# Global attention: softmax weights transposed in 32x32 blocks by VectorE and by DMA through DRAM, in place of TensorE

## The chip, the core and the metric

The kernel runs on one core of a Trainium2 chip. The metric is the device time of one execution in microseconds. The kernel before takes 859.36 us (median of 3 runs, 859.27 to 859.72). The core has TensorE (PE, its weight loads shown apart as PEld), VectorE (DVE), ScalarE (ACT), GpSimd (POOL) and SyncE (SP), which here issues nearly all DMAs. Each engine takes its instructions in one fixed order, and an instruction that waits holds up all behind it on that engine.

## The reference

Two layers of a hybrid encoder over 512 grid tokens and 16 meta tokens, width 1024. Each layer has one input projection, whose columns feed a global attention branch, a windowed attention branch, a gate for each, and two merge gates:

```python
def attend(qb):                                   # global branch: 8 heads, 2 kv heads, width 64
    s = jnp.einsum('bqkgd,bskd->bkgqs', qb, k).astype(jnp.float32) * scale
    p = jax.nn.softmax(s, axis=-1).astype(v.dtype)
    return jnp.einsum('bkgqs,bskd->bqkgd', p, v)
...
oa = gqa_attention(qa, ka, va) * jax.nn.silu(za)
ob = neighbourhood_attention(qb, kb, vb, rpb) * jax.nn.silu(zb)
ya = jnp.einsum('ble,ed->bld', oa, w_o_attn)
yb = jnp.einsum('ble,ed->bld', ob, w_o_na)
mixed = jax.nn.sigmoid(ga) * ya + jax.nn.sigmoid(gb) * yb
return x + jnp.einsum('bld,de->ble', mixed, w_out)
```

The change is in `attend`: between the softmax `p`, which has queries on the partitions, and the product with `v`, which needs the keys there.

## The kernel before, in words

Activations lie with features on the partitions and tokens along the free dimension. Every large product is done with three float32r matmuls: a value is split into a high part (a rounding copy) and a low part (what is left), and high x high, high x low and low x high are accumulated (lines 325 to 327 in `product`). A weight chunk comes in two halves of 256 KB. For each half SP loads `raw`, ACT casts it to `whi`, POOL subtracts to get `wlo`; each of the three has 4 buffers, so a load waits until POOL is done with the half four places earlier.

The projections and merge products are the main stream of TensorE. Attention work is threaded into it by two `Side` objects. `product` calls `tick()` after each of its spans (about 24 matmuls in layer 0); each tick moves the branches one step, and every fourth tick a new unit of global attention begins. So two or three units are in flight. `GQA_AT` says at which tick of a unit each step is emitted, for layer 0 and layer 1.

A unit of global attention is one head and 256 queries (two parts of 128): 16 units in each layer, and 2 in layer 0 for the 64 meta queries of a kv head. Its steps before:

- `scores(i)`: TensorE computes S (lines 556, 557), VectorE scales it, takes the maximum and writes it to SBUF (L807), ScalarE exponentiates (L811), VectorE multiplies by the reciprocal sum (L813). The weights P of a part are 128 queries x 528 keys, and both parts share the tile `both` of 1056 columns.
- `transposes(kt)`: four 128x128 transpositions on TensorE into a PSUM bank `pt` (L129), then `split`: ScalarE casts the bank to `pth`, VectorE subtracts to get `ptl` (L193, L194). Two such steps for a unit, 8 transpositions.
- `meta_transposes`: one narrow transposition of the 32 columns of meta keys into `ptm`, split by two casts and two subtractions into the padded tile `ga`.
- `sums`: 9 matmuls of `VA2` with `pth`, `ptl` and `ga` into `av` (L854).

`VA2` is V with tokens on the partitions: `scaled` writes V of all heads (`va`) from PSUM, and `values` transposes it.

The framework gives each instruction its place in its engine's queue by priorities and its own estimate of times, so the table sets the emission and the queue orders follow from it.

Of the kernel before, what the change touches and what calls it, by code (L numbers as in the profile page):

```python
# [11 lines left out]
F32 = mybir.dt.float32  # L12
# [6 lines left out]
P = 128  # L19
# [3 lines left out]
NREAL = GW * GH  # L23
# [13 lines left out]
GQA_AT = ({"scores": (0, 2), "transposes": (3, 4), "meta": 5, "sums": (5, 7)},  # L37
          {"scores": (0, 1), "transposes": (3, 6), "meta": 6, "sums": (5, 7)})
# [57 lines left out]
def trunk_kernel(ctx: ExitStack, tc: tile.TileContext, xT, w, gn, gf, bias, rope, out):  # L96
# [357 lines left out]
    for l in range(DEPTH):  # L454
# [264 lines left out]
        def values(v, out, tiles, name):  # L719

            n = tiles[0][2]
            ps = bank(ps_t, f"vt{name}", "tp")
            for i, (u, a, _) in enumerate(tiles):
                nc.tensor.transpose(ps[:n, P * i:P * (i + 1)], v[:, a:a + n], ident)
            u, e = tiles[0][0], len(tiles)
            src = ps[:n, :P * e].rearrange("p (t h d) -> p t h d", t=e, h=2)
            split(out[:n, u:u + e, :, 0], out[:n, u:u + e, :, 1], src)
            if n < P:
                nc.gpsimd.memset(out[:NMETA, u].rearrange("p h s d -> p (h s d)").bitcast(F32), 0.0)
                nc.scalar.copy(out[n:2 * n, u:u + e], out[:n, u:u + e].bitcast(F32))  # L730
# [15 lines left out]
        side_gqa.later(NORM_AT[l]["values"][1], lambda v=v, VA2=VA2: values(v, VA2, [(4, NTOK - 32, 64)], f"am{l}"))  # L746
# [68 lines left out]
        def global_unit(kv, parts, n, name, done):  # L815
# [41 lines left out]

            steps = [(at, lambda i=i: scores(i)) for i, at in zip(range(len(parts)), GQA_AT[l]["scores"])]
            n_t = 4 // per
            for i, (at, then) in enumerate(zip(GQA_AT[l]["transposes"][:n_t], GQA_AT[l]["sums"][-n_t:])):  # L860
                steps.append((at, lambda kt=per * i: transposes(kt)))
                f = 2 * per * (i + 1)
                steps.append((then, lambda a=2 * per * i, b=f + (f == 8): sums(a, b)))
            steps.append((GQA_AT[l]["meta"], meta_transposes))
# [391 lines left out]
```

## Time and profile before

| quantity | value |
|---|---|
| median of 3 runs | 859.36 us |
| the profiled execution: its time, its span | 859.04 us, 857.3 us |
| PE busy, share of the span | 847.7 us, 99% |
| PEld busy | 788.7 us, 92% |
| DVE busy | 533.7 us, 62% |
| ACT busy | 492.4 us, 57% |
| POOL busy | 352.7 us, 41% |
| mean granted TensorE clock | 0.998 |
| DMA moved | 95.55 MB in 64670 packets |
| queue q1, share of 16 DMA engines | 37.5% |
| PE's part in the chain that ended last | 93% |

The span runs from the first to the last instruction of the profiled execution; 1.7 us of its time lie outside. Busy time is the union of an engine's instructions. Matmuls overlap (one of 264 columns is shown as lasting some 0.29 us, and the next starts 0.12 us after it), so the cost of a matmul on PE is read from the distance between starts.

### The profile page before, as it was taken

What the parts mean: (1) busy time and instruction counts of PE and PEld (TensorE: products, weight loads), DVE (VectorE), ACT (ScalarE), POOL (GpSimd) and SP (SyncE); (2) the same over time, 40 slices, a digit from 0 to 9 for tenths busy, and PEclk for the clock granted to TensorE, in tenths of its full rate; (3) what the DMA queues carried; (4) which work ended last, traced back from release to release, by engine and by line L of the source; (5) the groups of instructions that cost most, each with busy time, mean ns of one, the idle gap of its engine ahead of it and who ended that gap; (6) DMA issues with size and microseconds to landing.
All of it is one profiled execution on the core that took longest, in us unless ns stands there. A gap on an engine that the chain in (4) does not pass through costs nothing.

```text
span 857.3 us, 16238 instructions
## 1 busy us (share of the span) xinstructions
PE 847.7 (99%) x5960; PEld 788.7 (92%) x5960; DVE 533.7 (62%) x1310; ACT 492.4 (57%) x1169; POOL 352.7 (41%) x279
## 2 busy tenths in 40 slices
PE   9999999999999999999999999999999999999997
PEld 9999999999999999999998999999988888888786
DVE  7975667777774673436448656677768545454633
ACT  8654777667864564334445556577758555543422
POOL 2663343333233233454764653334333333344851
PEclk9999999999999999999999999999999999999999
DMA  7384334335122212334655654334442222223502
GB/s 251 94 220 125 100 114 126 94 97 132 50 60 65 75 63 64 117 93 146 155 134 135 173 167 132 108 99 140 123 119 75 81 79 76 86 86 121 174 13 99
DMA packets 64670, 95.55 MB, mean 111 GB/s; under 512 B 22864, under 2 KB 23888, under 8 KB 64592
## 3 DMA queue, kind: packets, MB, share of 16 engines
q1 hardware_dynamic: 63872, 93.46, 37.5%
q8 instruction: 47, 0.77, 0.4%
q10 hardware_dynamic: 720, 1.06, 0.3%
q14 instruction: 31, 0.25, 0.1%
HBM read 76.72 MB, written 4.19 MB: 94 GB/s over the span
## 4 chain that ended last, share of the span: by engine, by line
PE 93%; ACT 3%; DVE 2%; issue 1%; DMA 1%; SPq 0%; POOLq 0%; POOL 0%; ACTq 0%; DVEq 0%
PE pp L327 19%; PE pp L325 19%; PE pp L326 19%; PE av L854 4%; PE y L327 4%; PE y L325 4%; PE y L326 4%; PE pt L129 3%; PE avb L997 2%; PE S L556 2%; PE S L557 2%; PE pf L1175 2%; PE pf L1177 2%; PE pf L1176 2%; PE Sb L557 1%
## 5 line engine op out<-in xcount | busy, mean ns | idle before, releaser
L241 POOL TENSOR_TENSOR wlo<-raw,whi 128x512 fp32r<-128x512 f32 x210 | 280.3, 1338 | 451.9 <-ACT whi L240 375.5
L325 PE MATMUL pp<-hh,whi 128*128 128x264 f32 (+1 forms) x1040 | 330.1, 317 | 0.0
L327 PE MATMUL pp<-hh,wlo 128*128 128x264 f32 (+1 forms) x1040 | 324.8, 312 | 0.0
L326 PE MATMUL pp<-hl,whi 128*128 128x264 f32 (+1 forms) x1040 | 323.9, 311 | 0.0
L240 ACT CAST whi<-raw 128x512 fp32r<-128x512 f32 x210 | 129.2, 619 | 151.8 <-issue 53.6
L327 PEld LDWEIGHTS pp<-hh,wlo 128*128 128x128 f32 x1040 | 195.8, 188 | 10.7
L326 PEld LDWEIGHTS pp<-hl,whi 128*128 128x128 f32 x1040 | 196.5, 189 | 9.0
L325 PEld LDWEIGHTS pp<-hh,whi 128*128 128x128 f32 x1040 | 196.1, 189 | 8.8
L807 DVE CUSTOM_DVE_ANT_1 P<-S,r 128x528 f32<-128x528 f32 x64 | 45.1, 705 | 18.5 <-PE S L557 17.5
L194 DVE TENSOR_TENSOR ptl<-pt,pth 128x512 fp32r<-128x512 f32 x64 | 44.0, 689 | 17.4 <-ACT pth L193 16.7
L1072 DVE TENSOR_TENSOR mg<-pp,rbc 128x264 f32<-128x264 f32 (+1 forms) x48 | 24.8, 517 | 41.9 <-PE pp L327 41.7
L811 ACT ACTIVATE P<-P,st 128x528 f32<-128x528 f32 x64 | 47.2, 737 | 2.0
L932 ACT ACTIVATE bias<-bias,stb 128x208 f32<-128x208 f32 (+1 forms) x64 | 31.1, 486 | 21.6 <-DVE stb L930 21.2
L193 ACT CAST pth<-pt 128x512 fp32r<-128x512 f32 x64 | 37.2, 583 | 4.4 <-PE pt L129 3.2
L129 PE MATMUL pt<-ident,P 128*128 128x128 f32 x256 | 39.2, 275 | 0.4 <-DVE ptl L194 0.4
L1073 ACT ACTIVATE mg<-mg 128x264 f32<-128x264 f32 (+1 forms) x48 | 23.7, 494 | 25.8 <-DVE mg L1072 25.8
L326 PE MATMUL pp<-mx,whi 128*128 128x264 f32 x128 | 36.6, 286 | 0.0
L325 PE MATMUL pp<-mx,whi 128*128 128x264 f32 x128 | 36.5, 285 | 0.0
L327 PE MATMUL pp<-mx,wlo 128*128 128x264 f32 x128 | 36.3, 284 | 0.0
L813 DVE TENSOR_SCALAR P<-P,st 128x528 f32<-128x528 f32 x64 | 34.1, 533 | 2.1
L854 PE MATMUL av<-pth,VA 128*128 128x256 f32 x128 | 35.4, 299 | 0.0
L854 PE MATMUL av<-ptl,VA 128*128 128x256 f32 x128 | 33.0, 280 | 0.0
(539 smaller groups left out, 1771.5 us busy)
## 6 DMA issues: line engine op xcount, KB each, us to landing
raw<-in_w_dram SPq DMA_DIRECT2D x210, 256.0 KB, 2.7
bias<-in_bias_dram SPq DMA_DIRECT2D x16, 480.0 KB, 4.2
KB<-KB SPq DMA_DIRECT2D x24, 272.0 KB, 3.7
rawl<-in_w_dram SPq DMA_DIRECT2D x16, 256.0 KB, 3.0
x<-in_xT_dram SPq DMA_DIRECT2D x8, 264.0 KB, 4.6
xr<-in_xT_dram SPq DMA_DIRECT2D x8, 264.0 KB, 3.7
Q<-q SPq DMA_DIRECT2D x16, 128.0 KB, 2.8
x1d<-xt SPq DMA_DIRECT2D x32, 64.0 KB, 3.0
```

What stands on the lines that cost most here:

```text
L129: nc.tensor.transpose(ps, src, ident[:n, :n])
L193: split_at["hi"] = nc.scalar.copy(hi, src)
L194: split_at["any"] = nc.vector.tensor_sub(lo, src, hi.bitcast(F32))
L240: cast = nc.scalar.copy(hi, raw)
L241: sub = nc.gpsimd.tensor_sub(lo, raw, hi.bitcast(F32))
L325: nc.tensor.matmul(ps, wh, rh[:, a:b], start=i == 0, stop=False)
L326: nc.tensor.matmul(ps, wh, rl[:, a:b], start=False, stop=False)
L327: nc.tensor.matmul(ps, wl, rh[:, a:b], start=False, stop=i == n - 1)
L807: newest["max"] = nc.vector.tensor_tensor_reduce(p[:n].rearrange("p (i k) -> p i k", i=2), S[:n, :, :HALF], scale[:n].unsqueeze(2).to_broa ...
L811: nc.scalar.activation(p[:n], p[:n], AF.Exp, bias=st[:n, 1:2], scale=1.0, accum_out=st[:n, 2:3])
L813: nc.vector.tensor_scalar_mul(p[:n], p[:n], st[:n, 3:4])
L854: nc.tensor.matmul(c["av"], rows2(c["t"][i][0]), c["t"][i][1], start=i == 0, stop=i == 8)
```

## The change

Each unit now does without TensorE between the softmax and `sums`:

- `turn(i)`: VectorE transposes part i within 32x32 blocks, in place (128x512 for part 0, 128x544 for part 1, which takes the 32 meta columns along; 64x544 for the meta queries, after a GpSimd memset of 16 columns). After part 1 SP stores the whole tile to DRAM (`there`, 540 KB, rows of 4224 bytes).
- `back`: SP loads it back into the same tile in four DMAs of 32 partitions each, in pieces of 512 bytes, so that blocks land on the partitions of their keys; a fifth DMA fetches the meta block (`meta`, pieces of 128 bytes).
- `split_part` and `split_ends` make `pth`, `ptl` and `ga` as before, but read SBUF in place of PSUM, `pth` and `ptl` through a view with runs of 32 elements.
- The keys come in another order, so `scaled` writes the columns of `va` permuted, with spans of 256 and 272 columns in place of 264 and 264, and the zeros for the meta values come with it (the memset in `values` goes).
- The table: in layer 0 `sums` moves from ticks (5, 7) to (6, 7), the two splits from (3, 4) to (5, 5); in layer 1 from (3, 6) to (5, 5).

```diff
-GQA_AT = ({"scores": (0, 2), "transposes": (3, 4), "meta": 5, "sums": (5, 7)},
-          {"scores": (0, 1), "transposes": (3, 6), "meta": 6, "sums": (5, 7)})
+GQA_AT = ({"scores": (0, 2), "turn": (1, 3), "back": 4, "split": (5, 5), "ends": 5, "sums": (6, 7)},
+          {"scores": (0, 1), "turn": (1, 2), "back": 3, "split": (5, 5), "ends": 5, "sums": (6, 7)})
...
         def scaled(c, name):
             t = slots.tile([P, 960], F32, tag="bias", bufs=2, name=name)
-            for ps, a, b in project(c, True):
-                evac["v"] = nc.vector.tensor_mul(t[:, a:b], ps, rbc[:, a:b])
-
-            nc.vector.tensor_mul(t[:, NTOK:NTOK + NMETA], ps[:, b - a - NMETA:b - a], rbc[:, NREAL:NTOK])
-            nc.gpsimd.memset(t[:, NTOK + NMETA:NTOK + 2 * NMETA], 0.0)
+            places = t[:, :NREAL].rearrange("p (k c j) -> p c k j", k=4, c=4)
+            nc.gpsimd.memset(t[:, NREAL:NREAL + 64], 0.0)
+            for ps, a, b in product(l, c, h, True, spans=((0, 2 * P), (2 * P, NTOK))):
+                i = a // P
+                s, r = (v.rearrange("p (c k j) -> p c k j", c=2, k=4) for v in (ps[:, :2 * P], rbc[:, a:a + 2 * P]))
+                evac["v"] = nc.vector.tensor_mul(places[:, i:i + 2], s, r)
+            for o in (NREAL, NREAL + 48):
+                nc.vector.tensor_mul(t[:, o:o + NMETA], ps[:, 2 * P:], rbc[:, NREAL:NTOK])
...
-            def transposes(kt):
-                tp = bank(ps_t, f"pt{name}_{kt}", "tp")
-                for i in range(per):
-                    for t, p in enumerate(c["p"]):
-                        o, k0 = width * i + n * t, first_token[t] + P * (kt + i)
-                        transposed(tp[:, o:o + n], p[:n, k0:k0 + P], n)
+            def turn(i):
+
+                a, b = (0, NREAL) if i == 0 and len(parts) > 1 else (NREAL * i, NREAL * i + NREAL + 32)
+                if len(parts) == 1:
+                    nc.gpsimd.memset(c["both"][:n, NTOK:b], 0.0)
+                nc.vector.transpose(c["both"][:n, a:b], c["both"][:n, a:b])
+                if i == len(parts) - 1:
+                    c["there"] = dpool.tile([P, 2 * (NREAL + 32)], F32, tag="turned", bufs=3, name=f"turn{name}")
+                    nc.sync.dma_start(c["there"][:n, :b], c["both"][:n, :b])
+
+            def back():
+
+                w, there = width * 4, c["there"][:n].rearrange("(b j) (t f) -> j t b f", j=32, t=2)
+                for q in range(4):
+                    r = slice(32 * q, 32 * q + 32)
+                    nc.sync.dma_start(c["both"][r, :w].rearrange("j (t b x) -> j t b x", t=len(parts), x=P),
+                                      there[:, :len(parts), :, P * q:P * q + P])
+                c["meta"] = tiny.tile([32, P], F32, tag="meta", name=f"pm{name}")
+                nc.sync.dma_start(c["meta"][:, :n].rearrange("j (b i) -> j b i", i=32),
+                                  c["there"][:n].rearrange("(b j) f -> j b f", j=32)[:, :, NREAL:NREAL + 32])
+
+            def split_part(kt):
+                v = c["both"][:, :width * 4].rearrange("p (x k i) -> p x k i", k=4, i=32)[:, :, kt:kt + per]
                 th, tl = slot("G", f"pth{name}_{kt}", F32R), slot("G", f"ptl{name}_{kt}", F32R)
-                split(th[:, :width * per], tl[:, :width * per], tp[:, :width * per])
+                split(*(t[:, :width * per].rearrange("p (k x i) -> p x k i", k=per, i=32) for t in (th, tl)), v)
...
-            def meta_transposes():
-                tp = bank(ps_t, f"ptm{name}", "tp")
-                rows = 32 * len(parts)
-                transposed(tp[:rows, :n], c["both"][:n, NTOK - 32:NTOK - 32 + rows], n)
-                tm = pad_tile("ga")
-                split_meta([(tm[:, n * t:n * (t + 1)], tp[:, :n]) for t in range(len(parts))])
+            def split_ends():
+
+                tm, m = pad_tile("ga"), c["meta"][:, :n]
+                with tc.high_priority():
+                    for t in range(len(parts)):
+                        nc.scalar.copy(tm[32 * t:32 * t + 32, n * t:n * (t + 1)], m)
+                    for t in range(len(parts)):
+                        nc.vector.tensor_sub(tm[64 + 32 * t:96 + 32 * t, n * t:n * (t + 1)], m, tm[:32, :n].bitcast(F32))
```

TensorE, layer 0, around the unit of head 2, first 256 queries (names end in `2_0`): in the order before, the two groups of transpositions `pt_2_0` and the `ptm_2_0` stand between main-stream matmuls (`pp`); the first group:

```order
L854 MATMUL av_1_1_2348<-ga_120,VA_768 128x256 [waits Activation_49]
L129 MATMUL pt_2_0_0_2483<-ident,P_2_0_2281 128x128 [waits DVE_49,PE_49]
L129 MATMUL pt_2_0_0_2483<-ident,P_2_0_2281 128x128 [waits DVE_49]
L129 MATMUL pt_2_0_0_2483<-ident,P_2_0_2281 128x128 x2
L325 MATMUL pp_24_264_2492<-hh_0_141,whi_24_0_2304 128x264
L326 MATMUL pp_24_264_2492<-hl_0_142,whi_24_0_2304 128x264
```

In the change TensorE has no `pt` and no `ptm` of these units; it goes on with the main stream until the first `av` of the unit, which stands after the first score matmuls of windowed head 4 (`Sb_4`) and waits for ScalarE's `pth`, then VectorE's `ptl`:

```order
L327 MATMUL pp_17_0_2667<-hh_7_230,wlo_17_1_2565 128x264
L556 MATMUL Sb_4_2694<-KB_20_2243,QB_2a 128x208 [waits DMAHW3_49,DMAHW7_49,DMAHW0_49,DVE_49]
L557 MATMUL Sb_4_2694<-KB_20_2243,QB_2a 128x208
L876 MATMUL av_2_0_2637<-pth_2_0_0_2597,VA_769 128x256 [waits Activation_49]
L556 MATMUL Sb_4_2694<-KB_20_2243,QB_2a 128x272
L557 MATMUL Sb_4_2694<-KB_20_2243,QB_2a 128x272
L556 MATMUL Sb_4_2694<-KB_20_2243,QB_2a 128x272
L557 MATMUL Sb_4_2694<-KB_20_2243,QB_2a 128x272
L556 MATMUL Sb_4_2694<-KB_20_2243,QB_2a 128x208
L876 MATMUL av_2_0_2637<-ptl_2_0_0_2598,VA_769 128x256 [waits DVE_49]
```

VectorE in the change, the same place: the softmax end and the block transposition of the next unit (`P_2_1`), then an evacuation of the main stream (`kb`), then the four splits of unit `2_0`, of which the first waits for four DMA queues:

```order
L815 RECIPROCAL st_2_1_1_2647<-st_2_1_1_2647 128x1 [waits Activation_49]
L816 TENSOR_SCALAR P_2_1_2529<-P_2_1_2529,st_2_1_1_2647 128x528 [waits DVE_49]
L838 STREAM_TRANSPOSE P_2_1_2529<-P_2_1_2529 128x544 [waits DVE_49]
L1076 TENSOR_TENSOR kb_3_2654<-pp_17_0_2667,rbc_411 128x64 [waits PE_49]
L1077 TENSOR_TENSOR kb_3_2654<-pp_17_0_2667,rbc_411 128x200
L194 TENSOR_TENSOR ptl_2_0_0_2598<-P_2_0_2270,pth_2_0_0_2597 128x8x2x32 [waits DMAHW4_49,DMAHW3_49,DMAHW5_49,DMAHW2_49,Activation_49]
L869 TENSOR_TENSOR ga_120<-pm_2_0_2527,ga_120 32x128 [waits DMAHW6_49,Activation_49]
L194 TENSOR_TENSOR ptl_2_0_2_2602<-P_2_0_2270,pth_2_0_2_2601 128x8x2x32 [waits Activation_49]
L869 TENSOR_TENSOR ga_120<-pm_2_0_2527,ga_120 32x128
L955 ISA bias_4_2595,stb_4_2695<-Sb_4_2694,bias_4_2595 128x208 [waits PE_49]
```

The block transpositions and the wait for DMA queues are new on VectorE; before, `ptl` waited for ScalarE alone.

SP in the change: the store of unit `2_0`, two weight loads (each waits for POOL), then the four loads back and the one of the meta block:

```order
L841 DMA turn_2_0_2480<-P_2_0_2270 128x1056 [waits DVE_49]
L235 DMA raw_21_0_2661<-in_w_dram 128x512 [waits DMAHW1_49,DMAHW0_49,Pool_49]
L235 DMA raw_21_1_2794<-in_w_dram 128x512 [waits DMAHW2_49,Pool_49]
L848 DMA P_2_0_2270<-turn_2_0_2480 32x8x128 [waits DMAHW7_49]
L848 DMA P_2_0_2270<-turn_2_0_2480 32x8x128 [waits DMAHW3_49]
L848 DMA P_2_0_2270<-turn_2_0_2480 32x8x128 [waits DMAHW4_49]
L848 DMA P_2_0_2270<-turn_2_0_2480 32x8x128 [waits DMAHW5_49]
L851 DMA pm_2_0_2527<-turn_2_0_2480 32x4x32 [waits DMAHW6_49]
L235 DMA raw_25_0_2800<-in_w_dram 128x512 [waits Pool_49]
```

These six DMAs are new in SP's order, for each unit; between store and return stand 0 to 3 weight loads or moves of windowed keys (`KB`), and weight loads are queued behind the return.

More of the change, by code (lines that the diff above doesn't have):

```diff
@@ L745, in trunk_kernel @@
         side_gqa.later(NORM_AT[l]["values"][0], lambda v=v, VA2=VA2: values(v, VA2, [(t, P * t, P) for t in range(4)], f"a{l}"))
[L746 removed]
+        side_gqa.later(NORM_AT[l]["values"][1], lambda v=v, VA2=VA2: values(v, VA2, [(4, NREAL, 64)], f"am{l}"))
         def silu_gate(tag, c, name):
@@ L858, in global_unit @@
             steps = [(at, lambda i=i: scores(i)) for i, at in zip(range(len(parts)), GQA_AT[l]["scores"])]
+            for i, at in zip(range(len(parts)), GQA_AT[l]["turn"][-len(parts):]):
+                steps.append((at, lambda i=i: turn(i)))
+            steps.append((GQA_AT[l]["back"], back))
             n_t = 4 // per
-            for i, (at, then) in enumerate(zip(GQA_AT[l]["transposes"][:n_t], GQA_AT[l]["sums"][-n_t:])):
-                steps.append((at, lambda kt=per * i: transposes(kt)))
+            for i, (at, then) in enumerate(zip(GQA_AT[l]["split"][:n_t], GQA_AT[l]["sums"][-n_t:])):
+                steps.append((at, lambda kt=per * i: split_part(kt)))
                 f = 2 * per * (i + 1)
                 steps.append((then, lambda a=2 * per * i, b=f + (f == 8): sums(a, b)))
-            steps.append((GQA_AT[l]["meta"], meta_transposes))
+            steps.append((GQA_AT[l]["ends"], split_ends))
             return sorted(steps, key=lambda x: x[0])
```

1 line of the change is left out of this document (removed).

## The prediction

> **What bounds the kernel now.** I read first the page's busy times and the chain of work that ended last:
>
> ```profile
> PE 847.7 (99%) x5960; PEld 788.7 (92%) x5960; DVE 533.7 (62%) x1310; ACT 492.4 (57%) x1169; POOL 352.7 (41%) x279
> PE 93%; ACT 3%; DVE 2%; issue 1%; DMA 1%; SPq 0%; POOLq 0%; POOL 0%; ACTq 0%; DVEq 0%
> L129 PE MATMUL pt<-ident,P 128*128 128x128 f32 x256 | 39.2, 275 | 0.4 <-DVE ptl L194 0.4
> ```
>
> TensorE is never free, and 93% of the chain is its own work. The waits of PE say the same: the longest in the whole span are
>
> ```profile
> PE warm L137 <- DVE one L143: 1.1, 1, 1.1
> PE tb L129 <- DVE ptl L194: 0.7, 1, 0.7
> ```
>
> So work taken off TensorE shortens the kernel, one for one, as long as nothing new makes it wait. What a transposition costs is read from the timeline of PE, by starts, since matmuls overlap:
>
> ```profile
> 301.08 0.29 PE L327 MATMUL pp<-hh,wlo 128*128 128x264 f32 x1
> 301.21 0.60 PE L129 MATMUL pt<-ident,P 128*128 128x128 f32 x4
> 301.57 0.37 PE L556 MATMUL S<-KA0h,Q 128*128 128x264 f32 x1
> 301.77 0.29 PE L557 MATMUL S<-KA0l,Q 128*128 128x264 f32 x1
> 301.90 0.28 PE L556 MATMUL S<-KA0h,Q 128*128 128x264 f32 x1
> ...
> 303.95 0.28 PE L854 MATMUL av<-ptl,VA 128*128 128x256 f32 x1
> 304.07 0.27 PE L129 MATMUL ptm<-ident,P 128*64 128x128 f32 x1
> 304.10 0.37 PE L325 MATMUL y<-ob,whi 128*128 128x264 f32 x1
> 304.30 0.28 PE L326 MATMUL y<-ob,whi 128*128 128x264 f32 x1
> ```
>
> A matmul of 264 columns starts 0.122 us after the one before it (301.08, 301.21; 301.77, 301.90). Four transpositions take 0.36 us, and the matmul behind them takes 0.20 in place of 0.12: 0.44 us for a group. A narrow one takes 0.03 and the same 0.08 behind it: 0.11 us.
>
> **What it removes from TensorE.** 256 `pt` are 64 groups: 64 x 0.44 = 28.2 us. 32 `ptm`: 3.5 us. The two units of meta queries have four and five small ones each, which at the same rates are about 0.8 us together. Sum 32.5 us. No matmul is added (the spans of V become 256 + 272 in place of 264 + 264). With nothing else the profiled execution, 857.3 us of span plus 1.7 us outside, would come to 859.0 - 32.5 = 826.5.
>
> **What it puts on the way of a unit.** The way from the last score matmul of a unit to its first `av` was: softmax, PE, ACT. It is now: softmax, block transposition, store to DRAM, four loads, ACT.
>
> ```profile
> 311.42 0.71 DVE L807 CUSTOM_DVE_ANT_1 P<-S,r 128x528 f32<-128x528 f32 x1 [0.25 <-PE S L557]
> ...
> 313.47 0.49 DVE L813 TENSOR_SCALAR P<-P,st 128x528 f32<-128x528 f32 x1
> ...
> L1136 DVE STREAM_TRANSPOSE xt<-xr 128x512 f32<-128x512 f32 x8 | 5.7, 711 | 0.3
> L193 ACT CAST pth<-pt 128x512 fp32r<-128x512 f32 x64 | 37.2, 583 | 4.4 <-PE pt L129 3.2
> L194 DVE TENSOR_TENSOR ptl<-pt,pth 128x512 fp32r<-128x512 f32 x64 | 44.0, 689 | 17.4 <-ACT pth L193 16.7
> bias<-in_bias_dram SPq DMA_DIRECT2D x16, 480.0 KB, 4.2
> out_dram<-y SPq DMA_DIRECT2D x4, 256.0 KB, 2.0
> Q<-q SPq DMA_DIRECT2D x16, 128.0 KB, 2.8
> Q<-Q SPq DMA_DIRECT2D x8, 128.0 KB, 3.8
> ...
> L535 SPq DMA_DIRECT2D KB<-KB x24: 461/467/598, 56.7 to 619.5; - x24
> ...
> DMA to landing us min/median/max: 2.9/3.7/5.8
> ```
>
> (The last two lines are from the view of the moves of windowed keys, `KB`, of 272 KB.) Softmax: from 311.42 to 313.96, 2.5 us, where nothing interferes, and 0.1 ahead of it. Transposition of 544 columns: 711 x 544/512 = 0.76. The store of 540 KB has no equal here: not under the 2.0 us of a 256 KB store, and by the 480 KB load at 4.2 us (it is nearest in size) about 4.5; I take 4.2. The loads back: SP issues the fourth 3 x 0.47 = 1.4 us after the first, and 128 KB land 2.8 to 3.8 us after issue: 4.2 to 5.2, I take 4.9. ACT's cast 0.6. Sum 2.6 + 0.8 + 4.2 + 4.9 + 0.6 = 13.1 us, if no queue holds any of it up. Pieces of 512 bytes are shown nowhere; this can only lengthen the 4.9.
>
> Queues do hold it up. In the order shown, between the softmax and the transposition of part 1, and ahead of the splits, VectorE has other work; for about half the units 3 to 8 instructions of 0.2 to 0.7 us stand before that transposition, some of which wait for a later matmul (0 to 4 us). On SP up to three weight loads stand between store and return, and SP spends its time waiting in front of just these:
>
> ```profile
> SPq L235 <- POOL wlo L241: 536.9, 186, 9.9
> ```
>
> 186 waits with a mean of 2.9 us. Part of that passes while the store is under way. So the way is 13 to 19 us, and I take 17 for the mean in layer 0, 16.5 in layer 1.
>
> **What the way may last.** In the change's PE order I counted the matmuls between the last score matmul and the first `av`. For head 0, first half, layer 0, these are 126 of 264 columns: 126 x 0.122 = 15.4 us. For layer 1 the long matmuls count by their own step:
>
> ```profile
> 612.66 0.39 PE L325 MATMUL pp<-hh,whi 128*128 128x512 f32 x1
> 612.89 0.39 PE L326 MATMUL pp<-hl,whi 128*128 128x512 f32 x1
> ```
>
> 0.23 us for 512 columns; head 5, second half: 67 x 0.23 + 17 x 0.12 = 17.5 us. The same count for all 34 units gives 15.3 to 21 us (one of meta queries 28): four are under 16, ten under 17, eighteen under 18, twenty-eight under 20. If every way lasted 16 us, what is missing adds up to 2 us; at 17, 9 us; at 18, 24; at 19, 43; at 20, 67. A stall at one `av` gives the same time to the unit behind it where its scores are already done, so less than that is paid. With ways of 16 to 19 us, spread, I charge 8 us.
>
> **What else waits.** ACT and VectorE wait in their own order for the loads back, with `whi` casts, exponentials and evacuations of the main stream (`kb`, `qb`, `mg`) behind them. The weights can bear it. SP waits 186 times for a free buffer (above), so the four `raw` are loaded ahead; ACT's `whi` waits until PE is done with an older half, POOL's `wlo` for ACT; no wait of `whi` for its load stands among the rows:
>
> ```profile
> POOL wlo L241 <- ACT whi L240: 375.5, 152, 16.3
> ACT whi L240 <- PE pp L326: 47.9, 50, 3.3
> ```
>
> The two PSUM banks of the main stream bear about one span (24 matmuls, 2.9 us) of VectorE's lateness. VectorE gets more to do: 64 transpositions of 0.71 to 0.76, 47 us; and its splits now take both inputs from SBUF. Such rows are
>
> ```profile
> L514 DVE TENSOR_TENSOR q<-q,Q 128x512 fp32r<-128x512 f32 x8 | 8.1, 1019 | 0.0
> L514 DVE TENSOR_TENSOR q<-q,Q x8: 670/865/1781, 38.3 to 479.5; 128x512 fp32r<-128x512 f32 x8
> L194 DVE TENSOR_TENSOR ob<-ob,ob 128x512 fp32r<-128x512 f32 x4 | 2.8, 690 | 0.4 <-ACT ob L193 0.3
> ```
>
> so a split lies between 0.69 (no change) and 1.02: 0 to 21 us for 64. I take half: the one form lies between 0.67 and 1.78 (minimum, maximum of the second line). The writes of V keep their size. VectorE rises from 534 to about 590 us, 71% of a span of 830. But not evenly:
>
> ```profile
> 115.00:145.00 30.00, 30.00 (x253) 29.42 (x251) 24.18 (x82) 23.30 (x69) 7.76 (x6) 1.00 0.35 105
> 205.00:235.00 30.00, 29.98 (x248) 29.00 (x247) 23.64 (x75) 23.82 (x69) 7.47 (x7) 1.00 0.26 75
> 570.00:610.00 40.00, 40.00 (x284) 37.36 (x283) 31.01 (x91) 29.44 (x79) 12.63 (x10) 1.00 0.46 134
> ```
>
> (columns: stretch, length, PE, PEld, DVE, ACT, POOL busy, clock, DMA share, GB/s.) At 1.8 units in 30 us and 1.8 us for a unit, 115 to 145 goes from 24.2 to 27.4 of some 29 us: 94%. An engine that full is late now and then by more than the banks bear; I charge 3 us for the three stretches.
>
> A page speaks against the change: the Trainium skill, VectorE: DVE Perf Modes, Rules for kernel authors, says to transpose 128x128 on TensorE where PSUM will do, and to use VectorE for 32x32. The trace's price for TensorE, 0.11 us, is far below VectorE's 0.7 for the four together with two DMA passes; by that rule the change loses, as in the last rival below, which is worked out from rows. On the other side, the Trainium skill, DMA: Bandwidth & Descriptors, Anatomy of one DMA, gives 2.0 us plus bytes at 436 GB/s: as an estimate 3.2 us for the store and 2.3 for a load, 2 us less for the way than I take, and then nearly all of it is hidden (826.5 + 4). The rows here, 4.2 us for 480 KB, are slower than that formula.
>
> **Sum.** 859.0 - 32.5 + 8 + 3 = 837.5; the median of the runs is 0.3 above the profiled execution: 838 us.
>
> **The rivals.**
>
> *All hidden.* The ways last 15 to 16 us and VectorE keeps up: 826.5 + 2 = 828. For it: the store row of 2.0 us. Against: DVE's orders above.
>
> *VectorE fills.* It becomes the bound in layer 0 from 60 to 235 us and in layer 1 from 490 to 610, some 295 us of the span. With splits at 1.02 and the subtractions of `ga` each held up too, a unit adds 2.5 us, and the 115 stretch goes to 24.2 + 4.5 = 28.7 of 29: every lateness then goes straight into PE. At 5% of 295 us, 15 us, beside the 8 of the ways: 850.
>
> *The round trip is too long: slower.* One mechanism: the return lands after the `av` is due in every unit. It decides from a mean way of about 18.5 us on, where what is missing (33 us) eats the whole 32.5. Price: KB moves land after 2.9 to 5.8 us; if the store takes 6 and the loads 1.4 + 5.8, the way is 2.6 + 0.8 + 6 + 7.2 + 0.6 = 17.2 without any queue and 19 to 20 with it: 43 to 67 missing, of which some two thirds are paid: 826.5 + 37 = 864. For it: 34.6 MB more (32 x 1.08) take the queue
>
> ```profile
> q1 hardware_dynamic: 63872, 93.46, 37.5%
> ```
>
> from 37.5% to 51% of the DMA engines. Against: the middle landing of the `KB` moves, 3.7, with the same neighbours.
>
> **How the numbers follow.** Forecast (832 to 846) 0.52; all hidden 0.17; VectorE fills 0.15; round trip too long 0.16. A measurement of this kernel tells 0.2%, 1.7 us, from no change: same is 857.6 to 861.1. Slower takes most of the last rival and nothing of the others: 0.14. Same 0.05, from between the last two. Faster 0.81. The range leaves out the best of "all hidden" and the worst of the round trip: 826 to 859.
>
> **What would show it.** Right: no `pt` on PE, PE's work about 32 us less; PE waiting for `av <- ACT pth` or `DVE ptl` some 5 to 15 us in all, mostly in layer 0; store landing near 4 us, loads near 3.5; DVE near 590. All hidden: those waits under 3 us. VectorE fills: PE waits for evacuations, on DVE, in 60 to 235. Round trip: waits over 30 us at `av`, and ACT idle for DMA ahead of `pth`. The forecast is wrong if stores or loads land after 6 us, or if the `whi` casts come to wait for their loads behind SP's new waits.

## The result and the profile after

The changed kernel takes 868.0 us (median of 4 runs, 866.0 to 869.8), beside 859.3 for the kernel before: a ratio of 1.010, 95% interval 1.007 to 1.013. Forecast were 838 us, range 826 to 859. It is slower by 8.7 us, outside the range. The profiled execution took 865.97 us, the fastest of the four; its span is 864.2.

From the page of the kernel after: busy times, then groups (busy, mean ns of one | idle time ahead and what ended it), then DMA queue and issues (KB each, median us to landing):

```profile
PE 827.5 (96%) x5662; PEld 758.5 (88%) x5662; DVE 591.3 (68%) x1378; ACT 489.1 (57%) x1169; POOL 354.3 (41%) x279
q1 hardware_dynamic: 108864, 128.64, 50.7%
L194 DVE TENSOR_TENSOR ptl<-P,pth 128x512 fp32r<-128x512 f32 x64 | 52.7, 824 | 12.7 <-ACT pth L193 12.1
L838 DVE STREAM_TRANSPOSE P<-P 128x512 f32<-128x512 f32 x64 | 46.3, 724 | 1.3
L193 ACT CAST pth<-P 128x512 fp32r<-128x512 f32 x64 | 39.3, 614 | 2.5 <-DMA P<-turn 1.5
turn<-P SPq DMA_DIRECT2D x32, 528.0 KB, 3.1
P<-turn SPq DMA_DIRECT2D x128, 128.0 KB, 3.1
```

Nearly every line that the prediction drew is there: no `pt` on PE, VectorE at 591 us (590 forecast), the queue at 50.7% (51%), stores and loads as fast as hoped or faster. And the page names one wait of ScalarE for a load back, 1.5 us: the data was nearly always in time. (For the store and a load, the Trainium skill's formula that the prediction quotes gave 3.2 and 2.3 us as estimates; its section there is on DMAs issued by GpSimd, these were issued by SP, and they landed after 3.1 and 3.1.) Yet PE is busy for 96% of a span that was to shrink. The waits of PE after (waits in us in total, times, longest):

```profile
PE av L876 <- DVE ptl L194: 5.9, 14, 1.0
PE av L876 <- ACT pth L193: 4.3, 6, 1.4
PE tb L129 <- DVE tal L194: 4.0, 2, 2.3
PE tc L129 <- DVE tal L194: 3.1, 2, 2.0
PE y L325 <- ACT oa_3a L193: 2.7, 2, 2.2
PE tb L129 <- DVE mm L990: 2.2, 1, 2.2
```

The lines speak of two places: `av`, where the prediction looked, and `tb`, `tc`, where it did not. A windowed head transposes its weights on TensorE into banks `ta`, `tb`, `tc` of the same two PSUM banks that `pt` used; each bank is split by ScalarE and VectorE (`tah`, `tal`) before it is free for the next but one.

These rows miss what is shorter than a wait, and matmuls overlap. So for all kernels here I took the distance between the starts of each two successive matmuls in the trace, less what that form takes when it is fed (0.126 us for 264 columns, 0.239 for 512, 0.115 for a transposition), and added up the excesses over 0.25 us: "lost steps". Before: 4.1 us. After: 37.2, of which 16.3 stand at `av` (26 steps), 15.2 at the windowed heads' matmuls and transpositions (13), 3.3 at `y`. Shorter excesses, steps near twice their length, rose from 1.6 to 5.6 us; more than half of them are a step of 0.22 us, in place of 0.12, from one `av` matmul to the next, most often right behind a wait. So -32.5 + 33.1 + 4.0 = +4.6, against +6.9 between the two profiled spans; 2.3 us stay unaccounted for.

One of the large losses, 136.4 to 139 us, from the timelines of PE, VectorE and POOL of the kernel after:

```profile
138.79 0.66 PE L129 MATMUL tb<-ident,bias 128*128 128x128 f32 x4 [2.31 <-DVE tal L194]
133.77 0.68 DVE L194 TENSOR_TENSOR ptl<-P,pth 128x512 fp32r<-128x512 f32 x1
134.48 1.67 DVE L869 TENSOR_TENSOR ga<-pm,ga 32x128 fp32r<-32x128 f32 x2
136.17 0.35 DVE L1080 TENSOR_TENSOR kb<-pp,rbc 128x184 f32<-128x184 f32 x1
136.44 1.40 DVE L194 TENSOR_TENSOR ptl<-P,pth 128x512 fp32r<-128x512 f32 x1
137.76 0.21 DVE L1081 TENSOR_TENSOR kb<-pp,rbc 128x64 f32<-128x64 f32 x1
138.06 0.67 DVE L194 TENSOR_TENSOR tal<-ta,tah 128x512 fp32r<-128x512 f32 x1
134.43 1.29 POOL L241 TENSOR_TENSOR wlo<-raw,whi 128x512 fp32r<-128x512 f32 x1 [5.00 <-PE tm L129]
136.02 1.27 POOL L241 TENSOR_TENSOR wlo<-raw,whi 128x512 fp32r<-128x512 f32 x1 [0.30 <-ACT whi L240]
```

`tal` could have run when its cast ended at 136.4. Ahead of it in VectorE's queue stand both splits of a global unit and its ends, a burst that took 3.75 us, and the evacuations of `kb`, which belong to the main stream. PE stands for 2.3 us, for a windowed head and not for the unit.

### The profile page after: what moved, and what is told of

Its sections match the earlier page's. It is cut to its first block, busy times and chain, and to the rows that moved or that the text cites. A ratio compares the mean times of both kernels' runs of the same rounds, so it can differ in the third digit from the quotient of the medians.

```text
span 864.2 us, 16032 instructions
## 1 busy us (share of the span) xinstructions
PE 827.5 (96%) x5662; PEld 758.5 (88%) x5662; DVE 591.3 (68%) x1378; ACT 489.1 (57%) x1169; POOL 354.3 (41%) x279
## 3 DMA queue, kind: packets, MB, share of 16 engines
q1 hardware_dynamic: 108864, 128.64, 50.7%
## 5 line engine op out<-in xcount | busy, mean ns | idle before, releaser
L325 PE MATMUL pp<-hh,whi 128*128 128x264 f32 (+3 forms) x1040 | 325.6, 313 | 0.3 <-DVE ma L1103 0.3
L327 PE MATMUL pp<-hh,wlo 128*128 128x264 f32 (+3 forms) x1040 | 325.1, 313 | 0.0
L326 PE MATMUL pp<-hl,whi 128*128 128x264 f32 (+3 forms) x1040 | 323.9, 311 | 0.0
L240 ACT CAST whi<-raw 128x512 fp32r<-128x512 f32 x210 | 129.0, 619 | 136.4 <-PE pp L326 43.3
L327 PEld LDWEIGHTS pp<-hh,wlo 128*128 128x128 f32 x1040 | 196.2, 189 | 10.5
L325 PEld LDWEIGHTS pp<-hh,whi 128*128 128x128 f32 x1040 | 196.1, 189 | 9.1 <-DVE ma L1103 0.5
L194 DVE TENSOR_TENSOR ptl<-P,pth 128x512 fp32r<-128x512 f32 x64 | 52.7, 824 | 12.7 <-ACT pth L193 12.1
L838 DVE STREAM_TRANSPOSE P<-P 128x512 f32<-128x512 f32 x64 | 46.3, 724 | 1.3
L876 PE MATMUL av<-ptl,VA 128*128 128x256 f32 x128 | 36.3, 305 | 6.2 <-DVE ptl L194 5.9
L876 PE MATMUL av<-pth,VA 128*128 128x256 f32 x128 | 37.3, 301 | 4.3 <-ACT pth L193 4.3
L193 ACT CAST pth<-P 128x512 fp32r<-128x512 f32 x64 | 39.3, 614 | 2.5 <-DMA P<-turn 1.5
L816 DVE TENSOR_SCALAR P<-P,st 128x528 f32<-128x528 f32 x64 | 37.1, 579 | 2.0
L327 PE MATMUL pp<-mx,wlo 128*128 128x264 f32 x128 | 36.3, 284 | 0.0
L325 PE MATMUL pp<-mx,whi 128*128 128x264 f32 x128 | 36.3, 284 | 0.0
```

The lines of the kernel that those rows point to most:

```text
L193: split_at["hi"] = nc.scalar.copy(hi, src)
L194: split_at["any"] = nc.vector.tensor_sub(lo, src, hi.bitcast(F32))
L240: cast = nc.scalar.copy(hi, raw)
L325: nc.tensor.matmul(ps, wh, rh[:, a:b], start=i == 0, stop=False)
L326: nc.tensor.matmul(ps, wh, rl[:, a:b], start=False, stop=False)
L327: nc.tensor.matmul(ps, wl, rh[:, a:b], start=False, stop=i == n - 1)
```

## The experiments

In the tables: the median, the ratio to the kernel before with its 95% interval, and the lost steps of the profiled execution.

### Taking the parts away

Three kernels leave out the block transpositions, the DMAs, or both:

```diff
-                nc.vector.transpose(c["both"][:n, a:b], c["both"][:n, a:b])      # no_turn, neither
...
-                    nc.sync.dma_start(c["there"][:n, :b], c["both"][:n, :b])     # no_dram, neither
...
-                    nc.sync.dma_start(c["both"][r, :w]...)                       # no_dram, neither: and the meta load
+                c["meta"] = c["both"][:32, :P]
```

`neither`: 

> Leaves out both the block transpositions and the round trip through DRAM: the splits read the unturned probabilities where the softmax left them, so the sums over V are of wrong numbers. TensorE's instructions are those of the changed kernel. Theory W (a unit's way through DRAM is late for its sums, and the in-order queues of ACT and VectorE hand the lateness on): the time falls to the floor of the prediction, 826.5 plus 2 to 6 us, 828 to 833. Theory V (VectorE has too much to do): the same, 828 to 833, since its 46 us of transpositions are gone. Theory G (the removed PE transpositions were worth less than the 32.5 us that I charged): it stays above 840.

`no_dram`: 

> Keeps the block transpositions on VectorE, leaves out the store and the loads: the splits read the block-transposed probabilities in place (wrong blocks, the same amount of work). Theory W: nearly all of the loss goes, 829 to 838 us. Theory V: the transpositions are still there, so 855 to 866. Where both bear, in between.

`no_turn`: 

> Keeps store and loads, leaves out the 66 block transpositions on VectorE (46 us of its time, and 0.7 us of each unit's way). Theory W: only 0.7 us of a way of some 18 us is gone, up to 10 us in all, so 856 to 866. Theory V: 46 us less on VectorE, 832 to 842.

| kernel | us | ratio | lost steps: at `av` / windowed heads / all | VectorE busy |
|---|---|---|---|---|
| before | 859.4 | | 0.4 / 1.9 / 4.1 | 533.7 |
| changed | 868.0 | 1.010 (1.007 to 1.013) | 16.3 / 15.2 / 37.2 | 591.3 |
| neither | 832.7 | 0.969 (0.967 to 0.970) | 0.4 / 8.7 / 11.6 | 550.8 |
| no_dram | 842.6 | 0.981 (0.979 to 0.982) | 0.4 / 16.1 / 19.6 | 591.0 |
| no_turn | 852.2 | 0.992 (0.990 to 0.993) | 9.9 / 12.1 / 25.3 | 555.9 |

The gain on PE is real: theory G falls, and 832.7 is the floor of 826.5 with 7.5 us more of lost steps. W and V, each alone, fall too: 10 us come with the transpositions, 19.5 with the round trip, 35 with both. But in what way does the round trip cost 20 us, if ScalarE hardly ever waits for its data?

### Is it the traffic?

`idle_trips` is `no_turn` with the loads moved behind the splits, which read the probabilities where they are:

```diff
-"back": 4 / 3
+"back": 6 / 6
-                tm, m = pad_tile("ga"), c["meta"][:, :n]
+                tm, m = pad_tile("ga"), c["both"][:32, :n]
```

> As `neither` (no block transpositions; the splits read the probabilities where the softmax left them), with the order of TensorE's and VectorE's instructions of `neither` to the last row, but every unit also makes its store and its five loads, of the same sizes and pieces, and nobody waits for what they bring. Theory T (the traffic itself costs: the weights come later through the same queue, or engines lose time to it): near the run without block transpositions, 845 to 852. Theory P (the traffic is free; what costs is where the splits now stand in the queues of ACT and VectorE, all at once just ahead of the sums and beside the windowed heads' own splits): as `neither`, 832 to 836.

832.4 us (0.967 to 0.970), lost steps 11.4. From its page:

```profile
PE 814.9 (98%) x5662; PEld 756.7 (91%) x5662; DVE 550.1 (66%) x1312; ACT 489.6 (59%) x1169; POOL 357.0 (43%) x281
q1 hardware_dynamic: 108864, 128.64, 51.3%
```

The same 128.64 MB in the same queue, and the time is that of `neither` to 0.4 us. The traffic is free here, also for the weights behind it on SP. What `no_turn` adds to this is that the splits depend on the loads, which it issues two or three ticks sooner, and so stand later in the queues of ScalarE and VectorE. In `neither`, by VectorE's timeline, a unit's split ran ten microseconds ahead of the windowed head's `tal` that comes next, and not right before it:

```profile
122.09 0.68 DVE L194 TENSOR_TENSOR ptl<-P,pth 128x512 fp32r<-128x512 f32 x1
132.04 0.69 DVE L194 TENSOR_TENSOR tal<-ta,tah 128x512 fp32r<-128x512 f32 x1 [0.78 <-ACT tah L193]
```

### More time for the way, or another place?

All of these are the changed kernel in full, with other ticks in the table:

```diff
-"split": (5, 5), "ends": 5, "sums": (6, 7)     # the changed kernel, both layers
+"split": (6, 6), "ends": 6, "sums": (7, 8)     # later1
+"split": (7, 7), "ends": 7, "sums": (8, 9)     # later2
+"split": (6, 7), "ends": 7, "sums": (7, 9)     # spread
+"split": (7, 8), "ends": 9, "sums": (9, 11)    # phase4
```

`later1`: 

> The changed kernel in full, with the splits and the sums of every unit one tick later (a tick is a span of the main stream, about 3.5 us): each way has about 3.5 us more. Theory W: with 17 to 20 us ways against allotments that rise from 15-21 to 19-24, most of the missing time is gone: 836 to 848. Theory V: VectorE's work is the same, 862 to 870.

`phase4`: 

> The changed kernel in full, with splits in ticks 7 and 8, ends in 9, sums in 9 and 11 of a unit, in both layers: exactly four ticks (one unit) after the transpositions and sums of the kernel before in layer 0, so in the same places of the windowed heads' rhythm, and one half at a time. Theory P: 836 to 848. Theory T and theory V (VectorE has too much to do): 862 to 872, since traffic and work are those of the changed kernel.

`later2`: 

> The changed kernel in full, both splits and the ends still in one tick, now tick 7, sums in 8 and 9: two ticks later than in the changed kernel and off the tick in which the windowed heads transpose. If only the distance to the windowed heads' splits matters, 840 to 850; if the burst of four splits at once matters by itself, 858 to 868; theories T and V: 862 to 872.

`spread`: 

> The changed kernel in full, splits in ticks 6 and 7, ends in 7, sums in 7 and 9: the two halves apart, the first in the tick of the windowed heads' transpositions. If the burst matters, 845 to 856; if the neighbourhood of the windowed heads does, 862 to 872, as one tick later with both at once (869.9); theories T and V: 862 to 872.

| kernel | us | ratio | lost steps: `av` / windowed / all |
|---|---|---|---|
| later1 | 869.9 | 1.011 (1.010 to 1.013) | 7.1 / 25.6 / 38.9 |
| spread | 866.4 | 1.008 (1.007 to 1.010) | 8.5 / 18.3 / 34.7 |
| later2 | 856.0 | 0.996 (0.995 to 0.998) | 6.0 / 15.3 / 29.9 |
| phase4 | 849.4 | 0.987 (0.986 to 0.989) | 2.5 / 13.9 / 22.8 |

`later1` refutes theory W: each way gets 3.5 us more, the loss at `av` falls from 16.3 to 7.1, and 10 us more appear at the windowed heads, in whose tick the splits now are. (Its layer 0, counted as in the table of stretches below, takes 318.4 + 83.0 us, beside 317.1 + 80.1.) `phase4` has the same work and traffic and takes 18.6 us less. So the place decides, theory P, though the time lies just above its range of 836 to 848. The guess about bursts is not borne out: `spread`, with the halves apart, is slow, and `later2`, with both at once in another tick, is between.

The other direction, the changed kernel's places in the kernel before:

```diff
-GQA_AT = ({"scores": (0, 2), "transposes": (3, 4), "meta": 5, "sums": (5, 7)},
-          {"scores": (0, 1), "transposes": (3, 6), "meta": 6, "sums": (5, 7)})
+GQA_AT = ({"scores": (0, 2), "transposes": (5, 5), "meta": 5, "sums": (6, 7)},
+          {"scores": (0, 1), "transposes": (5, 5), "meta": 5, "sums": (6, 7)})
```

> The kernel before, with TensorE's transpositions, no block transposition and no round trip, but with the changed kernel's places: transpositions and splits all in tick 5, sums in 6 and 7. Theory P (bunching the splits beside the windowed heads costs by itself): slower than before, 862 to 870. If the places of the changed kernel are harmless and only its waiting for data and VectorE's work cost: 858 to 861.

868.0 us, ratio 1.010 (1.008 to 1.011): the table alone makes the kernel before as slow as the changed one. Its PE waits now where two kinds of transpositions share two banks:

```profile
PE pt L129 <- DVE VB L194: 2.6, 4, 0.9
PE pt L129 <- DVE tbl L194: 1.7, 3, 0.9
PE tc L129 <- DVE tal L194: 1.4, 1, 1.4
```

(This one wait, `pt` for a bank, the changed kernel hasn't; the test says that these ticks are a bad place, not that the loss is the same one.)

### Two inputs from SBUF beside POOL

The mean `ptl` rose from 689 to 824 ns. By form and duration (min/median/max ns), before, then after:

```profile
L194 DVE TENSOR_TENSOR ptl<-pt,pth x64: 672/692/694, 70.2 to 755.7; 128x512 fp32r<-128x512 f32 x64
```

```profile
L194 DVE TENSOR_TENSOR ptl<-P,pth x64: 670/691/1744, 83.1 to 769.9; 128x512 fp32r<-128x512 f32 x64
```

The median is the same; a few take twice as long. Set beside POOL's subtractions in the trace (beside means an overlap of over 0.1 us): of 43 that ran without one, none was longer than 0.69 us; of 21 that ran beside one, 15 were longer than 0.8. Read from PSUM, in the kernel before, 28 ran beside POOL and none was slowed. The slow ones add 8.6 us, and the small subtractions into `ga`, slowed in 8 of 66 cases, 5.6 more. In `no_port` each subtraction became two instructions with one input:

```diff
-                split(*(... for t in (th, tl)), v)
+                    split_at["hi"] = nc.scalar.copy(hi, v)
+                    nc.vector.tensor_scalar_mul(lo, v, 2.0 ** -12)
+                    split_at["any"] = nc.vector.tensor_scalar_mul(tl[:, :160], th[:, :160].bitcast(F32), 2.0 ** -12)
```

> The changed kernel, but the low parts of the probabilities and of their ends are made by instructions with one input (a multiple of the high value) in place of a subtraction with two inputs from SBUF; each subtraction becomes two such instructions, so that VectorE keeps about the same time for them where nothing interferes (0.69 us). The sums over V are then of wrong low parts. Theory K (two-input subtractions from SBUF, 0.69 us alone and up to 1.74 in the trace where a weight subtraction of POOL runs beside them, add 14 us to VectorE in bursts, and TensorE pays for them): 852 to 862 us. Theory P alone (only the place in the queues counts): 864 to 870.

874.3 us (1.016 to 1.019), slower than both theories say. The instructions with one input are slowed as well (from its view of `ptl`):

```profile
L860 DVE TENSOR_SCALAR ptl<-P x64: 396/422/1517, 82.0 to 777.7; 128x512 fp32r<-128x512 f32 x64
L861 DVE TENSOR_SCALAR ptl<-pth x64: 226/243/1304, 83.8 to 778.5; 128x160 fp32r<-128x160 f32 x64
```

With twice as many to be caught, VectorE rose to 605 us. The experiment took the contention away nowhere, so it does not price it; it shows that 14 us more on VectorE, in the same places, cost 6.3 us of time. The Trainium skill, SBUF — State Buffer, Who interferes with whom, says that VectorE and GpSimd share a port pair that one instruction holds to its end, and names for VectorE both two inputs from SBUF and, for copies and tensor_scalar, a two-port mode. Rows and rule agree, for both forms; by this rule the kernel before was spared because its splits read PSUM.

### Tables without priority

`table_a` and `table_b` take the high priority from the units' splits, and spread the steps otherwise:

```diff
+"scores": (0, 1), "turn": (1, 2), "back": 2, "split": (5, 7), "ends": 7, "sums": (9, 9)     # table_a, layer 0
+"scores": (0, 1), "turn": (1, 2), "back": 2, "split": (5, 6), "ends": 6, "sums": (8, 8)     # layer 1
+"scores": (0, 2), "turn": (1, 3), "back": 3, "split": (8, 8), "ends": 8, "sums": (9, 11)    # table_b, layer 0
+"scores": (0, 1), "turn": (1, 2), "back": 2, "split": (7, 9), "ends": 10, "sums": (9, 12)   # layer 1
```

`table_a`: 

> The changed kernel in full with other places: both scores one tick apart (0 and 1), splits in ticks 5 and 7 (layer 0) and 5 and 6 (layer 1), sums in 9 and in 8, and without high priority for the unit's splits. From the phase4 run (849.4, 23 us of steps lost on TensorE, 14 of them at the windowed heads): if handing the queues back to the windowed heads removes a third of that, 842 to 847; if the sums, now at once, wait as before, 849 to 856.

`table_b`: 

> The changed kernel in full with splits in ticks 8 and 8 (layer 0), 7 and 9 (layer 1), sums in 9 and 11, 9 and 12, and without high priority for the unit's splits. Theory P with room enough: 842 to 848. If the end of layer 0, where the last unit's sums are needed at once, eats what the later places win: 849 to 855.

860.4 us (1.000 to 1.002) and 851.9 (0.990 to 0.993). Both miss their better case. `table_a` loses 20.9 us at the windowed heads and 3.0 at `av`: the sums had room, the heads did not. Neither is better than `phase4`. Priority and places changed together, so what the priority does alone is not shown.

### The end of layer 0, and a gain in another place

Where is what `phase4` still loses? The time that PE takes for stretches of the main stream, counted by its matmuls (L325 to L327), from the trace:

| main-stream matmuls | before | changed | neither | no_dram | phase4 | tail_early | phase4_shift |
|---|---|---|---|---|---|---|---|
| 1 to 1800 (most of layer 0) | 314.9 | 317.1 | 300.1 | 303.4 | 302.7 | 302.4 | 302.2 |
| 1800 to 2400 (its end) | 74.2 | 80.1 | 74.5 | 74.5 | 81.1 | 81.0 | 79.4 |
| 2400 to 3000 | 99.7 | 99.2 | 99.3 | 99.3 | 99.2 | 99.7 | 99.7 |
| 3000 to the last (layer 1) | 293.8 | 292.6 | 281.6 | 287.7 | 291.3 | 281.6 | 281.6 |

(The first row counts from the first of them, without the start.) `phase4` wins its time against the changed kernel in layer 0; at the end of that layer it loses 7 us against the kernel before. My reading was that the last unit's sums are wanted at once there, and that the way has nothing left to hide it. The timeline of PE in `phase4`:

```profile
340.89 0.29 PE L327 MATMUL y<-oa_2a,wlo 128*128 128x264 f32 x1
342.15 0.51 PE L325 MATMUL y<-oa_3a,whi 128*128 128x264 f32 x2 [0.98 <-ACT oa_3a L193]
342.90 0.39 PE L326 MATMUL y<-oa_3b,whi 128*128 128x264 f32 x1 [0.24 <-DVE oa_3b L194]
343.93 0.39 PE L325 MATMUL pp<-hh,whi 128*128 128x264 f32 x1 [0.28 <-DVE ma L1103]
```

So I gave the last two units of layer 0 an earlier table; `end_early4` the last four; `end_act` moved the division from VectorE to ScalarE besides:

```diff
+QUICK_AT = {"scores": (0, 2), "turn": (1, 3), "back": 4, "split": (6, 6), "ends": 6, "sums": (7, 8)}
+            at_of = QUICK_AT if name in ("0_7_0", "0_7_1") else GQA_AT[l]
...
-            nc.vector.tensor_scalar_mul(p[:n], p[:n], st[:n, 3:4])       # end_act, tail_act
+            nc.scalar.mul(p[:n], p[:n], st[:n, 3:4])
```

`end_early`: 

> The changed kernel in full with the table of `phase4`, but the last two units of layer 0 (head 7, both halves) in a table of their own: splits and ends in tick 6, sums in 7 and 8. In `phase4` the stretch of TensorE around the end of layer 0 (the 1800th to the 2400th matmul of the main stream) took 81.1 us, in the kernel before 74.2. Theory E (there the last unit's way has nothing left to hide it, and the later sums lengthen it): 843 to 847. If the end of the layer is not what is left: 848 to 851.

`end_early4`: 

> As `end_early`, with the last four units of layer 0 (heads 6 and 7) early, their scores in ticks 0 and 1. Theory E: 842 to 847. If their splits fall beside those of the windowed heads again: 848 to 852.

`end_act`: 

> As `end_early`, and in addition the probabilities are multiplied by one over their sum on ScalarE instead of VectorE (64 x 0.58 = 37 us less on VectorE, about 45 more on ScalarE, which is at 58%). Theory V2 (VectorE's 46 us of transpositions cost some 0.25 to 0.45 us of the span for each us, as the runs without them showed): 6 to 12 us less than `end_early`, if ScalarE's own queue doesn't give it back; if place and end of layer are all, no change.

842.1, 843.5 and 840.9 us (ratios 0.980, 0.981 and 0.978, each to 0.002). In these three the ends of some units are overwritten by the next unit's before their sums read them; the work is the same. With the ends in tick 7 (`"ends": 7`), where nothing is overwritten:

`tail_early`: 

> As `end_early`, with the ends of head 7's units in tick 7 in place of 6, behind the sums of the unit before them, so that a unit's ends no longer overwrite those of the unit before. Everything else in its place: 841 to 844 by theory E, as `end_early` (842.1).

`tail_act`: 

> As `tail_early`, with the division by the sums on ScalarE, as in `end_act` (840.9 beside 842.1): 839 to 842. Theory V2's 6 to 12 us did not show there; if they do not show here either, VectorE's load as such is not what is left.

841.3 us, ratio 0.980 (0.978 to 0.981), and 840.2, 0.978 (0.976 to 0.980). The time was as theory E said, and its reason was false: in the table of stretches the end of layer 0 keeps its 81.0 us, and the gain of 9.7 us stands in layer 1, whose units I had not touched. Counting the ticks of the program explains it: layer 0 ends with the units' count at 91 in `phase4` and, because the last units are shorter, at 88 in `tail_early`, while that of the windowed heads is 88 in both. Units begin at every fourth tick of their own count; so in layer 1 they begin one tick earlier against the heads. (`later1`, `later2`, `spread` and `table_a` shift layer 1 in this way too, by one or two ticks, so that each of those runs changed two things there; `phase4` does not.) The shift alone:

```diff
-GQA_AT_TICK, NA_AT_TICK = (0, 0), (1, 1)
+GQA_AT_TICK, NA_AT_TICK = (0, 3), (1, 1)
```

> The table of `phase4` for all units, with layer 1's units started one tick earlier against its windowed heads (three ticks later in the units' own count). `tail_early` was 8 us faster than `phase4`, but not where theory E put it: the stretch at the end of layer 0 kept its 81 us, and 9.6 us went in layer 1, whose units started one tick earlier against the heads because the shorter last table left the units' count three ticks lower. Theory P (only this shift did it): 839 to 844. Theory E (the early last units did it in some other way): 847 to 851, as `phase4`.

840.2 us (median of 5 runs, 839.8 to 842.5), ratio 0.979 (0.977 to 0.980). Layer 1 takes 281.6 us, to a tenth what it takes in `neither`, which has no round trip and no block transposition. The costliest wait in `phase4`, then the page and the waits of `phase4_shift`:

```profile
PE tc L129 <- DVE tal L194: 7.2, 6, 2.3
```

```profile
PE 817.4 (97%) x5662; PEld 756.2 (90%) x5662; DVE 584.5 (70%) x1378; ACT 488.9 (58%) x1169; POOL 355.7 (42%) x279
PE tc L129 <- DVE tal L194: 4.1, 4, 1.4
PE av L876 <- DVE ptl L194: 1.3, 3, 0.5
PE y L325 <- ACT oa_3a L193: 1.0, 1, 1.0
```

Up to 3.4 of the 9.7 us are two stretches of 3.4 us at half the clock in layer 1 of `phase4`, at 583 and 624 us, which are gone with the stalls before them. So in these places VectorE's load as such is not what costs, although it is still 51 us above the kernel before: `tail_act` takes 30 us from VectorE,

```profile
PE 819.7 (98%) x5662; PEld 758.6 (90%) x5662; DVE 553.0 (66%) x1312; ACT 532.2 (63%) x1235; POOL 353.4 (42%) x279
```

and wins 1.2 us, inside the scatter of the two. Of the 10 us of `no_dram` over `neither`, at least 6 were place too: it lost them in layer 1, where `phase4_shift` does not lose them with more to do.

`phase4_shift` and `tail_act` compute everything and beat both kernels. What is left to `neither`, 7.5 us, stands mostly at the end of layer 0 (79.4 against 74.5). The runs without the round trip do not have this loss (74.5 in `no_dram`); no run that keeps it mended it, and its cause stays open.

## Why the prediction was wrong, step by step

- **What bounds the kernel, and what TensorE gives up (32.5 us).** Right. PE was the bound; `neither` has the removal without block transpositions and round trip, in the places of the changed kernel, and reaches 832.7, which with its 7.5 us more of lost steps is 32.5 to within 1.3.
- **The way of a unit.** Right in sum. Store 3.1 us where I took 4.2; the four loads 1.9 us between first and fourth issue and 3.1 landing, where I took 4.9 for both. From the issue of the store to the last load landed the trace shows 8.9 us (median of 34 units), by my terms 9.1.
- **What is missing at `av`, 8 us.** Measured 16.3 of lost steps. The size is off by two, the mechanism more: I compared the way with what PE has to do in the meantime, as if ScalarE split the block when it came. It came 2.7 us (median) before ScalarE turned to it, and in three units only was ScalarE idle for it, 2.3 us in all. The lateness is the queue's: its order was laid out so that the split stood close ahead of the sums.
- **What else waits, 3 us: the step that failed.** I went through the weights, the evacuations and their two PSUM banks, and found that they bear it; they do. I did not go through the other user of the splits' place, the windowed heads: with `pt` gone, PE reaches `tb` and `tc` sooner and waits there instead (`neither`, without block transpositions and DMAs, already loses 8.7 us there; `before_late`, in the same ticks and with `pt`, loses 2.6 there and 7.8 at its own `pt` and `ptm`), and VectorE, in the same ticks, has a block transposition, two splits and the ends more in front of `tal`. This cost 15.2 us, the end of layer 0 some 6 (80.1 against 74.2, part of it among the steps at `av`), and the lowered clock in the profiled execution at most 1.7 (one stretch of 3.4 us at half rate). That the table moved the splits into tick 5 stood in the diff, and I read it only for what it allots to the way; in the kernel before it costs 8.5 us by itself.
- **VectorE.** 591 us for 590 forecast; splits from SBUF cost 8.6 us where I took half of 0 to 21. The 5.6 us at `ga` I did not see. The 94% that I read for the stretch from 115 us was the right warning, taken for 3 us.
- **The rivals.** *The round trip is too long* ended at 864, near the result and on its side, but by luck: its mark, ScalarE idle for the DMA, is nearly absent (2.3 us), and more time for the way (`later1`) did not help. *VectorE fills* named the engine at the bottom of most waits, but as a load; as a load it costs little (`tail_act`). *All hidden*, 828, is what `idle_trips` comes near to, with all of the traffic. My 838 is near what the same work takes in better places, 840.2, and that is luck too: of the 17.6 us of lost steps there, 3.2 stand at `av`, where I had 8.

## What to carry to other kernels

Where every engine takes its work in a fixed order, an edit that moves work from the bounding engine must be costed at each place where another stream waits behind the moved instructions, not only along its own path; look for the chains that share its engines and PSUM banks, here a windowed head's split. When a large edit gains nothing, first move its steps by a tick each way, relative to the other streams, and see whether the time follows: here 28 of 868 us hung on a table of numbers. A gain confirms a theory only if it appears in the stretch that the theory names.

## What the runs showed of the hardware

A stall of PE can cost more than its length. In the kernel after, a stall at 248.7 us (PE 1.01 busy of 3.20) was followed by 3.4 us at half the clock, of which the row shows 3.2: 16 matmuls, where a stretch as long that starts at 604.1 us has 29; one at 598.5 (0.92 of 2.90) was not (columns: PE, PEld, DVE, ACT, POOL busy, granted clock, DMA share, GB/s):

```profile
248.00:251.20 3.20, 1.01 (x8) 0.81 (x8) 3.04 (x7) 2.10 (x5) 2.42 (x2) 0.97 0.02 6
251.20:254.40 3.20, 3.20 (x16) 3.16 (x15) 1.87 (x6) 2.18 (x6) 0.16 (x2) 0.50 0.70 181
```

```profile
598.00:600.90 2.90, 0.92 (x5) 0.46 (x5) 2.48 (x6) 2.83 (x9) 0.00 (x0) 1.00 0.10 32
600.90:604.10 3.20, 3.20 (x20) 2.72 (x19) 3.08 (x8) 2.04 (x5) 1.03 (x1) 1.00 0.69 208
```

In `phase4`, at the end of layer 0, no single step was longer than 1.3 us, and the clock fell all the same after 8 us in which PE was busy for five:

```profile
336.00:339.50 3.50, 2.03 (x16) 1.64 (x14) 3.27 (x5) 1.45 (x4) 1.97 (x2) 1.00 0.20 75
339.50:344.00 4.50, 3.01 (x19) 2.37 (x19) 2.40 (x5) 1.38 (x3) 0.00 (x0) 1.00 0.17 58
344.40:347.60 3.20, 3.20 (x17) 3.20 (x16) 1.56 (x2) 0.63 (x1) 1.69 (x1) 0.50 0.13 35
```

What decided is seen in the traces' records of the granted clock. In each of the 20 kernels' traces all changes to half the clock lie whole multiples of 3.413 us apart, and each holds for one or two such windows (until the last matmuls of the span). I counted PE's busy share in every window of that grid, without the first 28 us and the last 15: all 14 windows with a share under 0.45 were followed by half the clock, 8 of those between 0.45 and 0.58, and none above. The stall at 248.7 us fell into one window, with a share of 0.29; the one at 598.5 was cut by a border into windows with 0.79 and 0.63; the broken stretch of `phase4` filled one to 0.56.

The Trainium skill, TensorE: Matmul & The Clock Gate, Part 1, has the half rate follow an idle window of about 3.4 us. The length of the windows here agrees; idle they need not be, since a window in which PE was busy for up to 0.58 of the time sufficed now and then. The mean granted clock was 0.990 to 0.997 in the runs of the changed kernel and 0.986 to 0.990 in those of `later1`, beside 0.998 to 1.000 in the kernel before. The times scatter more as well: 866.0 to 869.8 us, against 859.1 to 859.7.

And a queue whose packets take 51% instead of 37% of the time of 16 DMA engines, with 35.2 MB more, half of it loaded in pieces of 512 bytes, cost nothing that these runs can tell (`idle_trips` beside `neither`: 832.4 and 832.7).
